# A hybrid convolution and attention block: results stored from ScalarE's queue, loads spread out or issued earlier

## The chip, the cores and the metric

The kernel runs on one core of one Trainium2 chip. The metric is device time of the whole program in microseconds (us), here the median of three runs. Six things work at once: TensorE (PE, with its weight loads PEld), VectorE (DVE), ScalarE (ACT), GpSimd (POOL), the queue of SyncE (SP), which computes nothing and issues DMAs, and the DMA engines that carry the data. Every queue runs in order: an instruction that waits holds up all that stands behind it on the same queue.

## The reference

One block of a diffusion backbone over 2048 tokens of width 1024, with 256 context tokens. In short:

```python
mod = silu(c) @ w_ada + b_ada                    # shifts, scales and gates
h = rms_norm(x) * (1 + sc1) + sh1                # the context likewise
hy, q, k, v, og, gf, gb = split(h @ w_in)
s_f, s_b = final_states(context)                 # start of the recurrences
o = gla(q, k, v, gf, s_f) + reversed gla(..., gb, s_b)     # 4 heads, chunks of 64
y_gla = rms_norm(o) * silu(og)
x0, x1, v = split(short_conv(hy))
y_hy = x0 * (irfft(rfft(x1 * v) * spectrum(filter_mlp)) + bias * (x1 * v))
x = x + g1 * (concat(y_hy, y_gla) @ w_out)
h2 = rms_norm(x) * (1 + sc2) + sh2
x = x + g2 * (square(relu(h2 @ w_mlp1)) @ w_mlp2)
return rms_norm(x) * norm_final
```

The kernel computes all of it in float32 accuracy: matmul operands are split into a high part (`split`: a cast on ACT, line 227) and a low part (a subtraction on DVE, line 228), and three products are summed (lines 222 to 224).

## The kernel before

The work runs in stages, and what one stage hands to the next goes through DRAM tensors: `d_s` (the spectrum of the convolution filter), `d_kt`, `d_v`, `d_og`, `d_q` (per-head operands), `d_u`, `d_x0` (the convolution's inputs), `d_yt` (the mixed output, transposed), `d_h2` (the MLP's input), `d_m` (the MLP's hidden layer). Every DMA in the file, load or store, is issued with `dma = nc.sync.dma_start`, so they all stand on SP's queue in program order.

**Filter and context** (to about 230 us). `mod_dve` (line 425) computes the modulation vectors on DVE: for each of two rows it sums eight terms, and right behind them come the two small matmuls into `pmt` (line 439). `kernel_steps` makes the filter for each of two halves of 256 channels, first generating it (`gen`), then turning it into a spectrum in 16 steps: `fetch` (line 610) loads a table `dff` of the Fourier transform for every second step, `turn` multiplies (`pz`, `pu` line 633), and `second` copies the result to `ks` on ACT (line 636, two buffers) and stores it to `d_s` (lines 640 to 645). `context_steps` is interleaved with it by `run`, which merges streams of work by given costs.

**Projection** (to about 800 us), which fills the DRAM tensors.

**Convolution and attention** (about 800 to 1150 us), two streams merged by `run`: the convolution goes over two halves of the channels, per half a forward part (`uc`, `pa`, `pb`), 16 frequency steps that load `dff`, an inverse table `dfi` and parts of the spectrum `kr`, `ki` (lines 910 to 919), and an inverse part that ends with a product on DVE into `x0` (line 996) and a store of it (line 998). The attention goes over four heads: `load_kv` and `load_q` fetch a head's `kt`, `vv`, `dc`, `qi`, `ki` together after the first quarter of the head before; `outputs` (line 1099) loads the output gate `og` of a quarter and forms `oq` from it; `back` transposes it and stores `yg` (line 1137).

**Output projection**, whose second norm stores `tt` to `d_h2` (line 1309). **MLP, first phase** (1350 to 1950 us): 128 results `c` are formed on ACT and stored to `d_m` (line 1360). **MLP, second phase**: `load_w2` loads and splits a block of weights, `load_u` loads four rows of `d_m`, `split_u` splits them; the phase begins with:

```python
    for kb in range(4):
        load_w2(0, kb)
        if kb == 0:
            load_u(0, 0)
        split_u(0, 0, (kb,))
    load_u(0, 1)
```

Of the kernel before, what the change touches and what calls it, by code (L numbers as in the profile page):

```python
# [10 lines left out]
F32 = mybir.dt.float32  # L11
# [196 lines left out]
def hybrid_block(ctx: ExitStack, tc, a, out, dbg=None):  # L208
    nc = tc.nc
    dma = nc.sync.dma_start  # L210
    mm = nc.tensor.matmul
# [138 lines left out]
    with ExitStack() as ek:  # L350
# [201 lines left out]
        def kernel_steps():  # L552
            for hc in range(2):
# [3 lines left out]

                def gen(t):
                    r = 2 * t
                    pp = pt("pg")  # L560
# [49 lines left out]
                def fetch(t):  # L610
                    kk = 2 * t
                    if t % 2 == 0:
                        st["f", t // 2] = kt_("kd", "dff")
                        dma(st["f", t // 2][:], a["dft_f"][:, kk:kk + 4, :].rearrange("p k n -> p (k n)"))

# [11 lines left out]
                def second(t):  # L627
# [95 lines left out]
    def gates(tbs):  # L723
# [44 lines left out]
        def turn(t):  # L768
# [9 lines left out]
            for h in range(2):  # L778
                dma(d_kt[2 * j + h, :, 4 * tb:4 * tb + 4], kt[h][:])
# [39 lines left out]
    def load_kv(h):  # L819
        kt = pre.tile([P, 16, 2, 64], F32, tag="kt", bufs=1, name="kt")  # L820
        dma(kt[:], d_kt[h])
        vv = gpool(h).tile([P, 16, P], F32, tag="vv", bufs=1, name="vv")
        dma(vv[:], d_v[:, h * P:(h + 1) * P].rearrange("(b p) e -> p b e", p=P))
        heads[h, "kv"] = (kt, vv)
# [50 lines left out]
    def conv_steps():  # L875
        for hc in range(2):
# [29 lines left out]
            def k0(t):  # L906
# [7 lines left out]
                for h in range(2):  # L914
                    hs = slice(h * 64, (h + 1) * 64)
                    dma(kr[hs].rearrange("p (k c) -> p k c", k=2), d_s[kk:kk + 2, 0:64, cs].rearrange("k p c -> p k c"))
# [562 lines left out]
    for kb in range(4):  # L1479
        load_w2(0, kb)  # L1480
        if kb == 0:
            load_u(0, 0)
# [88 lines left out]
```

## Time and profile before

| | |
|---|---|
| time, median of 3 runs | 2693.38 us (2691.67 to 2700.61) |
| profiled execution, its own time | 2698.1 us |
| its span | 2696.3 us |
| mean granted TensorE clock | 0.972 |
| PE busy | 2549.9 us (95%) |
| DVE, ACT, POOL busy | 1384.1, 1045.7, 605.4 us |
| DMA | 353.53 MB, 131 GB/s over the span |

The busy table says which engine is nearest to the span. A row of a stretch has its length, the busy time of each engine with its instructions in brackets, the granted clock (1.00 is 2.4 GHz, 0.50 is 1.2 GHz), the share of the DMA engines and their GB/s; it says where PE isn't busy, and at which clock it ran. The table of waits names for each idle time the work that ended it. The timeline of a queue shows what stood in front of a DMA when it was issued late.

### The profile page before, as it was taken

What the parts mean: (1) busy time and instruction counts of PE and PEld (TensorE: products, weight loads), DVE (VectorE), ACT (ScalarE), POOL (GpSimd) and SP (SyncE); (2) the same over time, 40 slices, a digit from 0 to 9 for tenths busy, and PEclk for the clock granted to TensorE, in tenths of its full rate; (3) what the DMA queues carried; (4) which work ended last, traced back from release to release, by engine and by line L of the source; (5) the groups of instructions that cost most, each with busy time, mean ns of one, the idle gap of its engine ahead of it and who ended that gap; (6) DMA issues with size and microseconds to landing.
All of it is one profiled execution on the core that took longest, in us unless ns stands there. A gap on an engine that the chain in (4) does not pass through costs nothing.

```text
span 2696.3 us, 36126 instructions
## 1 busy us (share of the span) xinstructions
PE 2549.9 (95%) x13704; PEld 2123.2 (79%) x13704; DVE 1384.1 (51%) x2320; ACT 1045.7 (39%) x1863; POOL 605.4 (22%) x568
## 2 busy tenths in 40 slices
PE   9799999999998788899899999999989999999995
PEld 5678978898887677788788887888768888888884
DVE  5755356735567676734543336333344434443654
ACT  6464342225225455334555556555421101111112
POOL 2130231214112213133233233232100000000454
PEclk9899999999999798899999999999999999999998
DMA  5425434432547678656533334333252212221422
GB/s 194 149 78 173 130 129 141 140 113 94 177 149 196 188 214 217 195 171 205 181 108 114 106 114 139 110 114 114 78 183 78 78 48 94 78 79 47 149 98 82
DMA packets 200622, 353.53 MB, mean 131 GB/s; under 512 B 21876, under 2 KB 106744, under 8 KB 192384
## 3 DMA queue, kind: packets, MB, share of 16 engines
q1 hardware_dynamic: 200448, 351.22, 41.0%
q8 instruction: 108, 1.77, 0.3%
q14 instruction: 66, 0.54, 0.1%
HBM read 246.23 MB, written 104.93 MB: 130 GB/s over the span
## 4 chain that ended last, share of the span: by engine, by line
PE 75%; DVE 8%; DMA 7%; issue 4%; POOL 3%; ACT 3%; SPq 0%; POOLq 0%; DVEq 0%; ACTq 0%
PE ps L1340 21%; PE ps L223 7%; PE ps L222 7%; PE ps L224 7%; PE ph L222 3%; PE ph L224 3%; PE ph L223 3%; PE po L223 1%; PE po L224 1%; PE po L222 1%; POOL x L1541 1%; PE pv L222 1%; PE pv L223 1%; PE pv L224 1%; DVE ss L1078 1%
## 5 line engine op out<-in xcount | busy, mean ns | idle before, releaser
L222 PE MATMUL ps<-w2h,uh 128*128 128x512 f32 x1024 | 399.6, 390 | 11.0 <-ACT uh L227 11.0
L223 PE MATMUL ps<-w2l,uh 128*128 128x512 f32 x1024 | 399.2, 390 | 0.2 <-DVE w2l L228 0.2
L224 PE MATMUL ps<-w2h,ul 128*128 128x512 f32 x1024 | 399.1, 390 | 0.0
L1340 PE MATMUL ps<-bh,wh 128*128 128x512 f32 x896 | 352.2, 393 | 9.3 <-ACT wh L227 4.4
L1340 PE MATMUL ps<-bl,wh 128*128 128x512 f32 x896 | 351.6, 393 | 0.3 <-DVE bl L228 0.2
L1340 PE MATMUL ps<-bh,wl 128*128 128x512 f32 x896 | 350.6, 392 | 0.0
L228 DVE TENSOR_TENSOR wl<-raw,wh 128x512 fp32r<-128x512 f32 x217 | 176.7, 820 | 248.9 <-ACT wh L227 248.7
L1538 DVE TENSOR_TENSOR acc<-acc,ps 128x512 f32<-128x512 f32 x192 | 131.8, 686 | 268.2 <-PE ps L224 268.2
L222 PEld LDWEIGHTS ps<-w2h,uh 128*128 128x128 f32 x1024 | 192.8, 188 | 51.3 <-ACT uh L227 11.5
L223 PEld LDWEIGHTS ps<-w2l,uh 128*128 128x128 f32 x1024 | 192.8, 188 | 40.3 <-DVE w2l L228 0.6
L224 PEld LDWEIGHTS ps<-w2h,ul 128*128 128x128 f32 x1024 | 192.6, 188 | 40.4 <-DVE ul L228 0.2
L227 ACT CAST uh<-ur 128x512 fp32r<-128x512 f32 x128 | 70.2, 619 | 367.2 <-PE ps L223 362.4
L1340 PEld LDWEIGHTS ps<-bh,wh 128*128 128x128 f32 x896 | 169.3, 189 | 49.3 <-ACT wh L227 4.8
L227 ACT CAST wh<-raw 128x512 fp32r<-128x512 f32 x217 | 134.2, 623 | 187.3 <-PE ps L1340 152.5
L1340 PEld LDWEIGHTS ps<-bl,wh 128*128 128x128 f32 x896 | 169.7, 189 | 36.7 <-DVE bl L228 1.6
L1340 PEld LDWEIGHTS ps<-bh,wl 128*128 128x128 f32 x896 | 170.0, 190 | 35.5 <-DVE wl L228 0.2
L1547 POOL TENSOR_TENSOR acc<-acc,x 128x1024 f32<-128x1024 f32 x16 | 39.9, 2491 | 632.8 <-PE ps L224 588.4
L222 PE MATMUL ph<-hth,whi 128*128 128x512 f32 x384 | 150.9, 393 | 0.0
L224 PE MATMUL ph<-hth,wlo 128*128 128x512 f32 x384 | 149.6, 390 | 0.4 <-DVE wlo L228 0.4
L222 PE MATMUL pv<-whi,hth 128*128 128x264 f32 x512 | 146.7, 287 | 3.0 <-ACT whi L227 2.9
L223 PE MATMUL ph<-htl,whi 128*128 128x512 f32 x384 | 149.4, 389 | 0.0
L223 PE MATMUL pv<-wlo,hth 128*128 128x264 f32 x512 | 145.0, 284 | 0.3 <-DVE wlo L228 0.3
(282 smaller groups left out, 4980.1 us busy)
## 6 DMA issues: line engine op xcount, KB each, us to landing
d_m<-c SPq DMA_DIRECT2D x128, 256.0 KB, 2.3
ur<-d_m SPq DMA_DIRECT2D x32, 1024.0 KB, 5.3
raw<-in_w_dram SPq DMA_DIRECT2D x31, 1024.0 KB, 5.1
xt<-in_x_dram SPq DMA_DIRECT2D x32, 512.0 KB, 6.9
mwt<-in_wada_dram SPq DMA_DIRECT2D x64, 256.0 KB, 3.0
raw<-in_w_dram SPq DMA_DIRECT2D x32, 512.0 KB, 3.5
raw<-in_wi_vg_dram SPq DMA_DIRECT2D x20, 528.0 KB, 4.9
wada<-in_wada_dram SPq DMA_DIRECT2D x16, 512.0 KB, 7.2
```

Source lines behind the costliest of these rows:

```text
L222: mm(ps, lh, rh, start=first, stop=False)
L223: mm(ps, lh, rl, start=False, stop=False)
L224: mm(ps, ll, rh, start=False, stop=last)
L227: nc.scalar.copy(hi, src)
L228: dve.tensor_sub(lo, src, hi.bitcast(F32))
L1078: dve.scalar_tensor_tensor(ss[64:128, m - 1, :], ss[64:128, m, :], dc[64:128, m:m + 1], ss[64:128, m - 1, :], op0=ALU.mult, op1=ALU.add)
L1340: mm(ps[:], x_[:, sl], y_[:, j, :], start=start and i == 0, stop=stop and i == 2, skip_group_check=True)
L1538: dve.tensor_add(ac, ac, pp[:])
L1541: (dve if at == 31 and p == 3 else gps).tensor_add(x2[:, hs], x2[:, hs], ac)
L1547: gps.tensor_add(acc[:, tile, :], acc[:, tile, :], x2[:])
```

## The change

Five edits, all in the order and the place of DMAs, one also in the order of small matmuls. No arithmetic changes.

1. Stores of results that ACT (or, for `x0`, DVE) has made are issued from ACT's queue: `d_s` (36, four of them small), `d_kt` (16), `d_yt` (16 of `yg`, 4 of `x0`), `d_h2` (32), `d_m` (128), 232 in all. They leave SP's queue.
2. `mod_dve` puts the two matmuls of a row behind the fourth term of the next row. The first two `dff` tables of a half are loaded while its filter is still generated (steps 10 and 12).
3. A head's loads are spread: `kt` after the first quarter of the head before, `vv` behind the `back` that follows, `dc` and `qi` after the second quarter, `ki` behind the `back` that follows. In the convolution the two `kr` loads of a step now stand ahead of its two `ki`.
4. The output gate of a quarter is loaded at the end of the quarter before.
5. The second MLP phase issues its first two blocks of weights and its first `load_u` before the first split.

```diff
+    put_out = nc.scalar.dma_start
...
         def mod_dve(js):
+            ends = []
...
-                    for m in range(2):
-                        o = 4 * j + 2 * m + s
-                        mm(pmt[:, o:o + 1], ac[:, m * P:(m + 1) * P], ones[:, 0:1], start=True, stop=True)
+                        if k == 3 and ends:
+                            ends.pop()()
...
+                    ends.append(end)
+            ends.pop()()
...
                 def gen(t):
                     r = 2 * t
+                    if t in (10, 12):
+                        fetch(t - 10)
...
-                        dma(d_s0[:, cs], k3[127:128, 0, :])
+                        put_out(d_s0[:, cs], k3[127:128, 0, :])
                         dma(d_s[0, 127:128, cs], zrow[0:1, :])
-                        dma(d_s[0, 0:127, cs], k3[0:127, 0, :])
-                        dma(d_s[1, :, cs], k3[:, 1, :])
+                        put_out(d_s[0, 0:127, cs], k3[0:127, 0, :])
+                        put_out(d_s[1, :, cs], k3[:, 1, :])
                     else:
-                        dma(d_s[kk:kk + 2, :, cs].rearrange("k p c -> p k c"), k3)
-
-                yield from staged(16, fetch, turn, second, w=W["k_turn"])
+                        put_out(d_s[kk:kk + 2, :, cs].rearrange("k p c -> p k c"), k3)
+
+                yield from staged(16, lambda t: fetch(t) if t > 3 else None, turn, second, w=W["k_turn"])
...
-                dma(d_kt[2 * j + h, :, 4 * tb:4 * tb + 4], kt[h][:])
+                put_out(d_kt[2 * j + h, :, 4 * tb:4 * tb + 4], kt[h][:])
...
                 if h == 7:
-                    dma(d_yt[ct * P:(ct + 1) * P, :], x0[:])
+                    put_out(d_yt[ct * P:(ct + 1) * P, :], x0[:])
...
     def outputs(h, q):
         vv, qi, ki, ss = heads[h]
         at = heads[h, q // 2]
         b0 = q * 4
-        og = gp.tile([P, 4, P], F32, tag="og", bufs=2, name="og")
-        dma(og[:], d_og[b0 * P:(b0 + 4) * P, h * P:(h + 1) * P].rearrange("(b p) e -> p b e", p=P))
+        if (h, q) == (0, 0):
+            load_og(0, 0)
+        og = heads.pop((h, "og", q))
...
         heads[h, "o", q] = oq
+        if q < 3 or h + 1 < NH:
+            load_og(h + (q + 1) // 4, (q + 1) % 4)
...
-        dma(d_yt[DH + h * P:DH + (h + 1) * P, q * 512:(q + 1) * 512], yg[:])
+        put_out(d_yt[DH + h * P:DH + (h + 1) * P, q * 512:(q + 1) * 512], yg[:])
...
                 outputs(h, q)
+                if q < 2 and h + 1 < NH:
+                    (load_kv, load_q)[q](h + 1, 0)
                 yield W["outs"]
                 if last:
                     back(*last)
                     yield W["back"]
+                if q < 2 and h + 1 < NH:
+                    (load_kv, load_q)[q](h + 1, 1)
                 last = (h, q)
-                if q == 0 and h + 1 < NH:
-                    load_kv(h + 1)
-                    load_q(h + 1)
...
-            dma(d_h2[tb, kp][:, :, p * P:(p + 1) * P], t4)
+            put_out(d_h2[tb, kp][:, :, p * P:(p + 1) * P], t4)
...
-        dma(d_m[2 * n + i, :, tb * 1024 + j * 512:tb * 1024 + (j + 1) * 512], c[:])
+        put_out(d_m[2 * n + i, :, tb * 1024 + j * 512:tb * 1024 + (j + 1) * 512], c[:])
...
+    w2n = [load_w2(0, 0)]
+    load_u(0, 0)
+    w2n.append(load_w2(0, 1))
     for kb in range(4):
-        load_w2(0, kb)
-        if kb == 0:
-            load_u(0, 0)
+        w2n[kb]()
         split_u(0, 0, (kb,))
+        if kb < 2:
+            w2n.append(load_w2(0, kb + 2))
     load_u(0, 1)
```

**Place 1, SP's queue as the spectrum steps of the first half begin.** `xt` are token rows, the number behind a name tells tiles apart. Before:

```order
L325 DMA xt_872<-in_ctx_dram 128x1024
L640 DMA d_s0_58<-ks_855 1x256
L642 DMA d_s_57<-ks_855 127x256
L643 DMA d_s_57<-ks_855 128x256
L325 DMA xt_880<-in_ctx_dram 128x1024
L645 DMA d_s_57<-ks_898 128x2x256
L614 DMA dff_901<-in_dft_f_dram 128x512
L645 DMA d_s_57<-ks_913 128x2x256
L614 DMA dff_929<-in_dft_f_dram 128x512
```

and now:

```order
L326 DMA xt_872<-in_ctx_dram 128x1024
L326 DMA xt_880<-in_ctx_dram 128x1024
L571 DMA dff_901<-in_dft_f_dram 128x512
L326 DMA xt_2022<-in_x_dram 128x1024
L571 DMA dff_929<-in_dft_f_dram 128x512
L326 DMA xt_2030<-in_x_dram 128x1024
L571 DMA dff_957<-in_dft_f_dram 128x512
```

Five stores have left; the second `xt`, the next `dff` and a further `xt` stand directly behind one another.

**Place 2, SP's queue at the change from the first to the second half of the convolution.** From the load of `uc` on. Before:

```order
L828 DMA uc_9010<-d_u_65 128x2048
L1137 DMA d_yt_67<-yg_8697 128x512
L1104 DMA og_8899<-d_og_64 128x4x128
L910 DMA dff_9227<-in_dft_f_dram 128x512
L912 DMA dfi_9229<-in_dft_i_dram 128x512
L916 DMA kr_9231<-d_s_57 64x2x256
L917 DMA ki_9232<-d_s_57 64x2x256
L998 DMA d_yt_67<-x0_8541 128x2048
L823 DMA vv_8969<-d_v_63 128x16x128
```

and now:

```order
L842 DMA uc_9009<-d_u_65 128x2048
L924 DMA dff_9229<-in_dft_f_dram 128x512
L926 DMA dfi_9231<-in_dft_i_dram 128x512
L1120 DMA og_8805<-d_og_64 128x4x128
L930 DMA kr_9233<-d_s_57 64x2x256 x2
L930 DMA ki_9234<-d_s_57 64x2x256 x2
L930 DMA kr_9248<-d_s_57 64x2x256
L837 DMA vv_8971<-d_v_63 128x16x128
```

The store of `yg` and the store of `x0` are gone from between the loads. They stand on ACT's queue, which had here (`zy` are copies for the inverse part, `oq` the attention's):

```order
L980 COPY zy_8743<-py_8738 128x512
L980 COPY zy_8755<-py_8750 128x512
L980 COPY zy_8768<-py_8763 128x512
L1121 ACTIVATE oq_8794<-po_8777 128x512
L980 COPY zy_8810<-py_8805 128x512
```

and has now:

```order
L1163 COPY yg_8699<-pp_8694 128x512
L1164 DMA d_yt_67<-yg_8699 128x512
L994 COPY zy_8745<-py_8740 128x512
L994 COPY zy_8757<-py_8752 128x512
L994 COPY zy_8770<-py_8765 128x512
L1012 DMA d_yt_67<-x0_8543 128x2048
L1146 ACTIVATE oq_8794<-po_8777 128x512
L994 COPY zy_8812<-py_8807 128x512
```

The store of `x0_8543` now stands in front of the `oq` of the next quarter.

**Place 3, SP's queue between the two MLP phases.** Before:

```order
L1360 DMA d_m_70<-c_17015 128x512
L1360 DMA d_m_70<-c_17032 128x512
L1360 DMA d_m_70<-c_17048 128x512
L1459 DMA raw_17063<-in_w2_dram 128x1024
L1467 DMA ur_17069<-d_m_70 128x4x512
L1459 DMA raw_17075<-in_w2_dram 128x1024
L1459 DMA raw_17083<-in_w2_dram 128x1024
L1467 DMA ur_17099<-d_m_70 128x4x512
L1459 DMA raw_17091<-in_w2_dram 128x1024
L1487 DMA nf_17102<-in_norm_final_dram 128x1024
```

and now (`raw_16756` is the last block of first-phase weights):

```order
L1259 DMA raw_16756<-in_w1_dram 128x2048
L1487 DMA raw_17063<-in_w2_dram 128x1024
L1498 DMA ur_17065<-d_m_70 128x4x512
L1487 DMA raw_17067<-in_w2_dram 128x1024
L1487 DMA raw_17077<-in_w2_dram 128x1024
L1498 DMA ur_17099<-d_m_70 128x4x512
L1487 DMA raw_17085<-in_w2_dram 128x1024
L1521 DMA nf_17102<-in_norm_final_dram 128x1024
```

The last stores of the first phase, of which three are shown, no longer stand ahead of the second phase's first loads; `ur` is what `load_u` loads.

## Rows read from the trace of the kernel before

**Rows 1.** The page: busy time of the matrix engine, share of the span, instructions.

```profile
PE 2549.9 (95%) x13704; PEld 2123.2 (79%) x13704; DVE 1384.1 (51%) x2320; ACT 1045.7 (39%) x1863; POOL 605.4 (22%) x568
```

**Rows 2.** Stretches: length, busy time of PE, PEld, DVE, ACT, POOL; granted clock.

```profile
0.00:250.00 250.00, 222.39 (x1435) 172.54 (x1436) 142.48 (x288) 137.14 (x277) 56.25 (x67) 0.95 0.46 147
...
800.00:1150.00 350.00, 292.74 (x2619) 253.21 (x2618) 254.54 (x527) 172.01 (x307) 80.88 (x87) 0.90 0.72 198
...
1350.00:1950.00 600.00, 595.10 (x2586) 488.51 (x2586) 247.90 (x341) 334.18 (x571) 175.61 (x125) 0.99 0.32 110
1950.00:2000.00 50.00, 38.78 (x161) 31.21 (x160) 25.67 (x34) 17.20 (x25) 0.00 (x0) 0.90 0.68 236
```

**Rows 3.** Waits of PE: line, releaser, total us, times, longest us.

```profile
PE pu L938 <- DMA dff<-in_dft_f_dram: 12.7, 2, 8.6
PE ps L222 <- ACT uh L227: 11.0, 1, 11.0
...
PE pu L633 <- DMA dff<-in_dft_f_dram: 9.2, 4, 7.7
PE pd L1063 <- DMA vv<-d_v: 8.2, 1, 8.2
...
PE pc L535 <- DVE ke L527: 6.8, 3, 5.0
...
PE pmt L439 <- DVE ac L435: 4.6, 3, 3.5
...
PE pp L1134 <- DVE oq L1126: 2.4, 1, 2.4
...
PE pa L888 <- DMA uc<-d_u: 1.8, 1, 1.8
```

**Rows 4.** SP's queue in time order: start us, length us, line, DMA.

```profile
94.67 2.28 SPq L643 DMA_DIRECT2D d_s<-ks  x1
...
97.99 0.42 SPq L614 DMA_DIRECT2D dff<-in_dft_f_dram  x1
...
914.93 0.58 SPq L828 DMA_DIRECT2D uc<-d_u  x1
941.78 0.33 SPq L1137 DMA_DIRECT2D d_yt<-yg  x1
...
949.77 0.33 SPq L998 DMA_DIRECT2D d_yt<-x  x1
...
1957.09 0.37 SPq L1467 DMA_DIRECT2D ur<-d_m  x1
```

**Rows 5.** ACT in time order; in brackets its idle time before, and the releaser.

```profile
103.49 0.59 ACT L636 COPY ks<-pu 128x512 f32<-128x512 f32 x1 [4.68 <-DMA d_s<-ks]
...
200.55 0.59 ACT L636 COPY ks<-pu 128x512 f32<-128x512 f32 x1 [3.69 <-DMA d_s<-ks]
...
948.44 0.60 ACT L1121 ACTIVATE oq<-po 128x512 f32<-128x512 f32 x1 [2.25 <-PE po L1118]
...
1955.23 0.63 ACT L1359 ACTIVATE c<-c 128x512 f32<-128x512 f32 x1
1960.59 1.04 ACT L227 CAST w2h<-raw 128x1024 fp32r<-128x1024 f32 x1 [4.73 <-DMA raw<-in_w_dram]
1964.18 2.18 ACT L227 CAST uh<-ur 128x512 fp32r<-128x512 f32 x4 [2.55 <-DMA ur<-d_m]
```

**Rows 6.** The chain of waits: start us, length us, what.

```profile
97.99 7.96 DMA dff<-in_dft_f_dram
...
192.93 7.55 DMA d_s<-ks
...
889.90 8.40 DMA dff<-in_dft_f_dram
```

**Rows 7.** Waits of SP's queue, in the same form as rows 3.

```profile
SPq L998 <- DVE x L996: 21.1, 4, 9.3
```

**Rows 8.** One stretch of the attention stage, columns as in rows 2.

```profile
920.00:930.00 10.00, 9.39 (x44) 8.90 (x44) 7.11 (x18) 2.79 (x6) 0.00 (x0) 0.50 0.23 91
```

More of the change, by code (lines that the diff above doesn't have):

```diff
@@ L436, in mod_dve, with end @@
                         yield 0.33
-                    for m in range(2):
-                        o = 4 * j + 2 * m + s
-                        mm(pmt[:, o:o + 1], ac[:, m * P:(m + 1) * P], ones[:, 0:1], start=True, stop=True)
+                        if k == 3 and ends:
+                            ends.pop()()
+                    def end(ac=ac, o=4 * j + s):
+                        for m in range(2):
+                            mm(pmt[:, o + 2 * m:o + 2 * m + 1], ac[:, m * P:(m + 1) * P], ones[:, 0:1],
+                               start=True, stop=True)
+                    ends.append(end)
+            ends.pop()()
         def mod_end():
@@ L556, in kernel_steps, with fetch @@
                 st = {}
+                def fetch(t):
+                    kk = 2 * t
+                    if t % 2 == 0:
+                        st["f", t // 2] = kt_("kd", "dff")
+                        dma(st["f", t // 2][:], a["dft_f"][:, kk:kk + 4, :].rearrange("p k n -> p (k n)"))
                 def gen(t):
                     r = 2 * t
+                    if t in (10, 12):
+                        fetch(t - 10)
                     pp = pt("pg")
@@ L817, in hybrid_block, with load_kv @@
     gpool = lambda h: gp if h % 2 else pre
[L819 to L824, printed above, removed]
+    def load_kv(h, part=None):
+        if part != 1:
+            kt = pre.tile([P, 16, 2, 64], F32, tag="kt", bufs=1, name="kt")
+            dma(kt[:], d_kt[h])
+            heads[h, "kt"] = kt
+        if part != 0:
+            vv = gpool(h).tile([P, 16, P], F32, tag="vv", bufs=1, name="vv")
+            dma(vv[:], d_v[:, h * P:(h + 1) * P].rearrange("(b p) e -> p b e", p=P))
+            heads[h, "kv"] = (heads[h, "kt"], vv)
     def load_u(ct):
@@ L913, in k0 @@
                 kr, ki = ft("kr", 5, "kr"), ft("ki", 3, "ki")
-                for h in range(2):
-                    hs = slice(h * 64, (h + 1) * 64)
-                    dma(kr[hs].rearrange("p (k c) -> p k c", k=2), d_s[kk:kk + 2, 0:64, cs].rearrange("k p c -> p k c"))
-                    dma(ki[hs].rearrange("p (k c) -> p k c", k=2), d_s[kk:kk + 2, 64:128, cs].rearrange("k p c -> p k c"))
+                for t_, q in ((kr, 0), (ki, 64)):
+                    for h in range(2):
+                        dma(t_[h * 64:(h + 1) * 64].rearrange("p (k c) -> p k c", k=2),
+                            d_s[kk:kk + 2, q:q + 64, cs].rearrange("k p c -> p k c"))
                 if t == 0:
@@ L1035, in hybrid_block, with load_q @@
             gps.memset(az[i][d][:], 0.0)
[L1037 removed]
+    def load_q(h, part=None):
         hr = slice(h * 64, (h + 1) * 64)
[L1039 to L1041 removed]
+        if part != 1:
+            dc = gp.tile([P, 32], F32, tag="dc", bufs=2, name="dc")
+            qi = gp.tile([P, T], F32, tag="qi", bufs=2, name="qi")
+            heads[h, "d"] = (qi, dc)
+        if part != 0:
+            ki = gp.tile([P, T], F32, tag="ki", bufs=1, name="ki")
+            heads[h, "q"] = (heads[h, "d"][0], ki, heads[h, "d"][1])
         for d in range(2):
             ds_ = slice(d * 64, (d + 1) * 64)
[L1044 to L1047 removed]
+            if part != 1:
+                dma(dc[ds_, :], d_dec[d, hr, :])
+                dma(qi[ds_, :], d_q[d, hr, :])
+            if part != 0:
+                dma(ki[ds_, :], d_ki[d, hr, :])
     def states(h):
```

21 lines of the change are left out of this document (7 added, 14 removed).

## The prediction

> **What bounds the kernel now.** The busy table comes first: PE is busy 2549.9 us of a span of 2696.3 [rows 1], so all idle time of PE together is about 146 us, and the change leaves PE's work alone. The stretches come second: they show where those 146 us lie [rows 2]. The first MLP phase (1350 to 1950 us) leaves 4.9 us idle of 600, so a queue that is faster there is worth nothing. The filter stage leaves 27.6 us of 250, the convolution and attention stage 57.3 us of 350 at a granted clock of 0.90, the seam between the MLP phases 11.2 us of 50. Only there can the change pay. The waits of PE come third, since they say what ends each idle time [rows 3]: the tables `dff` (12.7 and 9.2 us), the operands of the second MLP phase (11.0), a head's `vv` (8.2), `ke` (6.8), `pmt` (4.6), `oq` for a transposition (2.4), `uc` (1.8). The timeline of SP's queue and the chain come last: they say whether such a load was late because it was issued late (the change can help) or because its bytes came late (it can't).
>
> **The change part by part.** The sum is made against the profiled execution (2698.1 us, span 2696.3), which lies 4.7 us above the median of 2693.38; I take the saving off the median.
>
> *`mod_dve`.* PE waits 3.5 us at the longest, 4.6 in three waits, for `ac` [rows 3]. The matmuls now come four terms later, so PE's other work can go first. But DVE is the one that is behind, and what needs the sums still waits for them. Between 0 and 3.5 I take 1.5: the wait is moved rather than removed.
>
> *Stores of `d_s`, tables ahead.* Two places. At 94.67 us SP spends 2.28 us to issue a `d_s` store, and the next `dff` is issued at 97.99 [rows 4]; it needs 7.96 us to land [rows 6], and PE waits 7.7 [rows 3]. In the new order the load stands behind two `xt` only (place 1), so it can go some 2.5 us sooner, and no stores are in front of it. Against that, the 2.28 us are now spent by ACT, which has evictions and casts to do there, and `ks` waited 4.68 us for a store's landing, until 103.49 [rows 5]: that is late next, and it bounds the gain at 105.95 (97.99 + 7.96) - 103.49, about 2.5 us, unless the store lands sooner as well. I take 3, with ends -1 and 7.7. At 200.55 ACT has waited 3.69 us for a store to free `ks` [rows 5]; that store was issued at 192.93 and took 7.55 us [rows 6]. `ke` stands behind this eviction on ACT, which gives PE's wait of 5.0 us [rows 3]. The store can start a little sooner, behind its own eviction, and no table is in front of it on its queue. I take 2.5, with ends -1 (ACT's issue time) and 5.0. PE ran at half the clock (0.50) for a while after idle time, as 920 to 930 us shows in the attention stage [rows 8]; each microsecond of it costs PE about half a microsecond. Two microseconds less of it behind these two waits, which is my estimate, are 1 us, with ends 0 and 3.
>
> *Heads' loads, gates and `yg`/`x0` stores.* SP stands still from 915.5 us, when `uc` has been issued, until 941.78, when the `yg` store goes [rows 4]. Behind it stand `og`, `dff`, `dfi`, `kr`, `ki` (place 2). That is 26 us of lead for these loads, but little of it was waited for: the only waits that it explains are `uc` (1.8 us; a head's operands that were held back are loaded beside it) and `oq` (2.4 us, its gate was issued late) [rows 3]. I take 1.8 and 1.5, with lower ends of 0. The great wait, 8.6 us for `dff` [rows 3], is one of bytes: the table was issued at 889.90 and took 8.40 us to land [rows 6], behind a head's `qi` and `ki`. Half of that head's bytes now come later, but they come ahead of the next table, and the number of bytes in this stage, in which the DMA engines are busy 0.72 of the time on average [rows 2], is the same. I take 2, with ends 0 and 8.6. `vv` (8.2) stays where it was, behind the last `ki`; one store less is ahead of it, 0.6 us.
> The price is on ACT. The store of `x0` was issued at 949.77, when DVE had finished; it now stands ahead of an `oq` that ran at 948.44 (place 2) [rows 4, 5]. So that `oq` and the copies behind it start at 949.77 + 0.33, 1.7 us late, and PE's products for the inverse part wait for these copies. The cover is the double buffer of `zy`. I take -1, with ends -2.5 and 0.
>
> *`d_kt`, `d_h2`, `d_m`.* A store of 256 KB costs its queue about 0.33 us [rows 4]. 128 for `d_m` are 42 us on ACT, which is busy 334 of the 600 us there [rows 2] and becomes 376: hidden under PE, 0. SP's long waits for `c` disappear, but no load behind them was late. The output projection has the same trade on a smaller scale: 0, with ends -2 and 0.
>
> *The seam of the MLP.* The last `d_m` stores stood ahead of it on SP, so the first `ur` went out at 1957.09 [rows 4], and PE started 11.0 us late [rows 3]. In place 3 the weights, `ur` and the next weights wait only for buffers that are freed ahead of the first phase's last products, so the data lies there when ACT comes: last square at 1955.23 + 0.63, a store (0.33), the cast of the weights (1.04), the first cast of `ur` (2.18 / 4 = 0.55) [rows 5]: 1955.86 + 0.33 + 1.04 + 0.55 = 1957.8. In the trace the first cast of `ur` started at 1964.18, so it ended at 1964.7: 6.9 us gained. What is late next are the third and fourth weights: they reuse the two buffers, so they can go out only after the first splits, and PE may stand there once more for 1 to 2 us. I take 5, with ends 2 and 7.
>
> Sum: 1.5 + 3 + 2.5 + 1 + 1.8 + 1.5 + 2 + 0.6 - 1 + 0 + 5 = 17.9 us. 2693.4 - 17.9 = 2675.5, rounded to **2675 us**. With the upper ends of all terms (3.5 + 7.7 + 5 + 3 + 1.8 + 2.4 + 8.6 + 0.6 + 0 + 0 + 7 = 39.6) it would be 2654, with the lower ends (0 - 1 - 1 + 0 + 0 + 0 + 0 + 0.6 - 2.5 - 2 + 2 = -3.9) 2697.
>
> The Trainium skill speaks against the stores' new queue: "DMA: Bandwidth & Descriptors", section "Issuing engines are not separate DMA queues", says that DMAs of all issuing engines end on the same 16 DMA engines and interleave, so that issuing on several engines saves only the time to initiate them. By that rule taken literally the stores would be worth 0.33 us each on a queue that PE does not wait for. The trace agrees on the bytes (8.40 us for a table, behind a head's operands) but not on the saving, because 26 us at the `yg` store are a wait for data in front of the issue, and not an initiation.
>
> **The rivals.** *Bytes, not queues.* The loads that PE waits for were limited by what the DMA engines carry and by DVE, and an earlier issue only lets them wait in another place. For it: 8.40 us for a table, `ks` waiting for landings. Against it: the seam, where nothing else was moved by the DMA engines for want of an issue. Then only `mod_dve` at 1.5 and the seam at its lower end of 2 remain: 2693.4 - 3.5 = 2690, within 0.3%. The Trainium skill's rule above would give this outcome.
> *ACT's queue becomes the place where others are held.* ACT is in order; where a store on it waits for DVE or for an earlier DMA that shares its completion counter, the evictions behind it wait too, and PE waits for those. Place: the four `x0` stores and the filter's `d_s` stores. Price: SP waited 21.1 us in four `x0` stores [rows 7], and the slow `d_s` issue of 2.28 us comes once in each half of the filter (4.6), together 25.7 us; the gains of the filter and the attention stage are then gone, and 1.5 and 5 remain. 2693.4 + 25.7 - 6.5 = 2712.6 if all of it reaches PE. It is slower by more than 0.3% (8.1 us) from 14.6 us of held time on. Against it: at the store that I could follow, ACT is held 1.7 us, since it comes late to the store by itself.
> *The clock comes back.* If the 8.6, 7.7 and 5.0 us waits shrink so far that the clock isn't halved after them, the upper ends hold: about 2654, and with the ten microseconds at half speed around 925 us gone (half of it, 5 us) 2649. For it: 0.50 in a stretch in which PE is busy 9.39 of 10 us [rows 8]. Against it: that stretch stands behind a full DMA system.
>
> **How the numbers follow.** The forecast (2660 to 2685) gets 0.60, bytes 0.18, ACT's queue 0.10, the clock 0.12. A measurement of this kernel tells about 0.3% from no change, 8.1 us. Forecast and clock are faster by more than that: 0.72; bytes are the same: 0.18; ACT's queue is slower: 0.10. The range of 2657 to 2692 leaves out most of the clock case and ACT's queue.
>
> **What would show it.** In the changed kernel's trace PE's wait ahead of the second MLP phase should be 4 to 6 us, with ACT in place of the `ur` load as releaser chain; the wait for `dff` near 106 us 3 to 5 us; that for `ke` near 203 us 2 to 3; `uc` and `oq` gone; `vv` still about 8; SP without a wait for `yg`. ACT's longest wait ahead of an eviction should be about 2 us behind the `x0` store. It is wrong if waits of PE for ACT appear that rows 3 doesn't have, or if the `dff` waits keep their size.

## The result, and the profile after

The changed kernel takes 2719.95 us (median of four runs, 2715.25 to 2721.11) against 2693.86 us for the kernel before, measured beside it: ratio 1.0089, 95% interval 1.0068 to 1.0111. It is **slower by 26 us**; the forecast was 2675, with a range of 2657 to 2692. The profiled execution of after (2721.11 us, span 2719.3) can be set against that of before (span 2696.3): 23.0 us.

On the page of after PE is busy 14.0 us longer than before [rows 1] with the same 13704 matmuls, and ACT's DMA ring (q10) carries 62.93 MB that SP's (q1) carried before:

```profile
PE 2563.9 (94%) x13704; PEld 2133.1 (78%) x13704; DVE 1377.3 (51%) x2320; ACT 1047.3 (39%) x1863; POOL 608.5 (22%) x568
...
q1 hardware_dynamic: 151228, 288.29, 33.5%
q10 hardware_dynamic: 49220, 62.93, 6.6%
```

So only 9.0 of the 23.0 us are idle time of PE; the other 14.0 are the same matmuls run more slowly, since the mean granted clock fell from 0.972 to 0.966. Stretches that hold nearly the same matmuls show both in each of the three stages that lose (columns as in rows 2). Filter, attention, output projection before:

```profile
0.00:335.00 335.00, 306.52 (x2093) 252.44 (x2094) 177.62 (x351) 169.19 (x335) 76.63 (x99) 0.96 0.45 144
840.00:1160.00 320.00, 262.96 (x2425) 227.94 (x2424) 232.66 (x466) 155.16 (x278) 80.88 (x82) 0.89 0.73 204
1160.00:1365.00 205.00, 196.26 (x909) 160.68 (x908) 100.04 (x136) 94.13 (x175) 71.91 (x55) 0.98 0.58 184
```

and after:

```profile
0.00:347.00 347.00, 311.95 (x2089) 257.25 (x2090) 176.65 (x350) 168.53 (x333) 79.30 (x98) 0.94 0.43 139
852.00:1179.00 327.00, 269.21 (x2424) 231.28 (x2422) 227.51 (x466) 154.67 (x278) 81.42 (x82) 0.87 0.68 200
1179.00:1394.00 215.00, 199.54 (x910) 163.14 (x909) 98.00 (x136) 94.74 (x176) 70.75 (x57) 0.96 0.54 175
```

PE's idle time (length less busy time) grew by 6.6 us in the filter, 0.8 in the attention stage and 6.7 in the output projection, its busy time by 5.4, 6.3 and 3.3.

To place the whole loss I matched PE's matmuls of the two traces one by one and took how much later each starts than in before; the median of these lags at the end of a stage, less that at the end of the stage before, is what the stage lost, by waits and by the clock together. The same was done for every kernel below:

```
us lost (+) or won (-)   filter   projec-  conv. and  output    1st MLP  seam
against before           to 330   tion     attention  project.  phase
after                     11.8    -0.4       7.3        9.8       1.0    -6.2
ds_on_sp                   0.9    -0.2       1.4       10.0       2.6    -6.0
split127                   3.0    -0.2       4.8        8.9       1.2    -6.1
yt_on_sp                  11.2    -0.8      -6.4        7.6       2.5    -6.3
x0_on_sp                  13.8     0.1       0.8        6.5       2.5    -6.1
yg_on_sp                   8.7    -0.4      -0.2        7.6       2.5    -6.3
h2_on_sp                  12.4     0.2      -1.0        1.3       1.1    -6.2
h2_t7_sp                  11.3     0.1       4.9        4.1       1.1    -6.2
h2_half                   13.4     0.9      -2.8        4.6       2.4    -6.3
combo                     -0.2     0.6      -6.6        1.4       2.3    -6.3
all_sp                     5.4     1.1     -10.1        0.3      -0.1    -0.4
dm_only                    1.9    -1.8     -10.9        0.5       1.4    -6.4
dm_late                    3.4    -3.4      -6.8       -0.8      -1.7    -6.3
b_dm                       1.3     0.5       1.1        0.4       2.3    -6.2
b_w2                       1.6     3.5      -3.2       -0.3      -0.3    -0.9
b_kv                       0.0     0.8      -7.5       -0.6      -0.2    -1.3
kv_late                    5.2    -1.0      -7.3        2.5      -0.1    -6.1
```

Each row is one profiled execution. Kernels whose code is the same in a stage show its scatter: up to 6 us in the filter, 7 in the projection, 10 in the attention stage, 4 or less in the others. A figure is therefore read over all kernels that share the code, and a verdict rests on the timed ratios. The profiled execution of `kv_late` is the longest of its five (2691.50 us at a granted clock of 0.969; the median is 2680.71, and the shortest had 0.977).

PE's waits in after (columns as in rows 3, to be read against them):

```profile
PE pu L952 <- DMA dff<-in_dft_f_dram: 13.8, 4, 7.1
PE ps L1332 <- DVE x L1316: 9.6, 4, 4.7
PE pc L544 <- DVE ke L536: 9.4, 3, 7.4
...
PE pd L1082 <- DMA vv<-d_v: 6.6, 1, 6.6
PE ps L1368 <- ACT wh L228: 5.7, 2, 5.3
PE pp L1161 <- DVE oq L1151: 5.6, 3, 3.2
PE pz L632 <- ACT tt L342: 5.4, 1, 5.4
```

The wait for `dff` in the filter (9.2 us in rows 3) has fallen to 0.3; 5.4 us for ACT's `tt` are new, and `ke` has grown from 6.8 to 9.4. `oq` has grown from 2.4 to 5.6, and the wait at line 1332 (4.1 us at the same place in before) is 9.6.

### The profile page after: what moved, and what is told of

The parts are those of the page before. It is cut to its first block, busy times and chain, and to the rows that moved or that the text cites. A ratio compares the mean times of both kernels' runs of the same rounds, so it can differ in the third digit from the quotient of the medians.

```text
span 2719.3 us, 35891 instructions
## 1 busy us (share of the span) xinstructions
PE 2563.9 (94%) x13704; PEld 2133.1 (78%) x13704; DVE 1377.3 (51%) x2320; ACT 1047.3 (39%) x1863; POOL 608.5 (22%) x568
## 3 DMA queue, kind: packets, MB, share of 16 engines
q10 hardware_dynamic: 49220, 62.93, 6.6%
## 4 chain that ended last, share of the span: by engine, by line
PE 48%; DVE 3%; POOL 3%; DMA 2%; issue 2%; ACT 1%; SPq 0%; POOLq 0%; ACTq 0%; DVEq 0%
PE ps L1368 21%; PE ps L224 8%; PE ps L223 8%; PE ps L225 8%; PE po L224 1%; PE po L225 1%; PE po L223 1%; POOL x L1575 1%; DVE bl L229 1%; DMA raw<-d_h 1%; DMA raw<-in_w_out_dram 0%; DMA d_h<-tt 0%; DVE x L1574 0%; POOL x L1311 0%; POOL mrs L277 0%
## 5 line engine op out<-in xcount | busy, mean ns | idle before, releaser
L225 PE MATMUL pv<-whi,htl 128*128 128x264 f32 x512 | 145.5, 285 | 0.2 <-DVE htl L344 0.2
```

The lines of the kernel that those rows point to most:

```text
L225: mm(ps, ll, rh, start=False, stop=last)
```

## The experiments

### The filter: `d_s` stores

ACT in after, in time order (start us, length us; ACTq rows are DMA issues):

```profile
98.65 0.21 ACTq L653 DMA_DIRECT2D d_s<-ks  x1
98.90 7.47 ACTq L654 DMA_DIRECT2D d_s<-ks  x1
106.42 0.78 ACT L342 ACTIVATE tt<-xp,mod,scl 128x512 f32<-128x512 f32 x1 [7.01 <-issue]
```

The issue behind the store of 127 rows takes 7.47 us, and ACT does nothing else in that time; PE gets its next `pz` operand right after, and then runs at 1.2 GHz (granted 0.51 from 110 to 120 us): four `pu` matmuls take 2.08 us, where they took 1.03 ahead of the wait:

```profile
100.87 1.03 PE L644 MATMUL pu<-zt,dff 128*128 128x256 f32 x4
107.25 1.11 PE L632 MATMUL pz<-prm,zk 128*128 128x128 f32 x4 [5.35 <-ACT tt L342]
108.31 2.08 PE L644 MATMUL pu<-zt,dff 128*128 128x256 f32 x4
```

On SP the same issue had taken 2.28 us [rows 4], and no evictions stood behind it. First run: only the 36 `d_s` stores go back to SP.

```diff
-                        put_out(d_s0[:, cs], k3[127:128, 0, :])
+                        dma(d_s0[:, cs], k3[127:128, 0, :])
...
-                        put_out(d_s[kk:kk + 2, :, cs].rearrange("k p c -> p k c"), k3)
+                        dma(d_s[kk:kk + 2, :, cs].rearrange("k p c -> p k c"), k3)
```

> The changed kernel with the 36 stores of d_s back on SP, all else as changed. Theory A (ACT is held by issuing these stores: one issue took 7.47 us on ACT, and matched matmuls fall behind by 12 us between 85 and 140 us): about 12 us come back, 2720 -> 2708, and the matmuls of the first spectrum steps stand within 2 us of the kernel before. Rival B (the loads brought ahead, xt and dff, take the DMA engines and land late): the 12 us stay, 2718 to 2722.

Measured: 2709.54 us, ratio 1.0052 (1.0032 to 1.0072). The filter loses 0.9 instead of 11.8. The early tables win nothing here: PE's longest wait for `dff` is 7.4 us (7.7 in rows 3), that for `ke` 5.0 as before.

```profile
PE pu L644 <- DMA dff<-in_dft_f_dram: 8.1, 2, 7.4
```

Second run: the stores stay on ACT, and only the one of 127 rows is cut in two.

```diff
-                        put_out(d_s[0, 0:127, cs], k3[0:127, 0, :])
+                        [put_out(d_s[0, r0:r1, cs], k3[r0:r1, 0, :]) for r0, r1 in ((0, 112), (112, 127))]
```

> The changed kernel, but the store of 127 rows of 1 KB, which stands ahead of the slow issue, is cut into 112 and 15 rows, on ACT as changed. Theory A1 (the 127 rows are carried by few of the DMA engines, and the next store's issue on ACT waits for them): the issue behind it falls from 7.47 us to under 1.5, and 6 to 8 us come back, 2712 to 2714. Rival A2 (the issue is slow because the DMA engines are full of loads, whatever the shape): the issue stays over 4 us and the time at 2718 to 2722.

Measured: 2707.42 us, ratio 1.004 (1.0025 to 1.0055), lower than the 2712 to 2714 expected. The issue behind it takes 0.36 us, and the filter loses 3.0:

```profile
97.60 0.81 ACTq L653 DMA_DIRECT2D d_s<-ks  x2
98.75 0.78 ACT L342 ACTIVATE tt<-xp,mod,scl 128x512 f32<-128x512 f32 x1 [0.39 <-DVE htl L344]
98.75 0.36 ACTq L654 DMA_DIRECT2D d_s<-ks  x1
```

So most of the filter's loss is this one shape of store, twice in the program (in the second half the issue takes 1.57 us, and `ke` is 7.45 us late, against 5.0 [rows 3]), and not the number of stores on ACT. With the store cut, the waits for `dff` and `ke` do shrink, to 3.1 and 2.9 us at the longest, but one for `kn` stands beside them (1.0 us in before):

```profile
PE pu L644 <- DMA dff<-in_dft_f_dram: 5.3, 2, 3.1
PE pk L600 <- DVE kn L588: 5.1, 2, 3.3
```

ACT's ring tells why the shape matters. In after, from 102 to 106 us, it moved

```profile
q10 hardware_dynamic: 40, 0.04, 2.9%
```

40 packets of 1 KB in 4 us; with the cut store, from 100 to 102 us,

```profile
q10 hardware_dynamic: 140, 0.12, 17.5%
```

140 in 2 us, seven times the rate. The Trainium skill states the rule behind it, in "DMA: Bandwidth & Descriptors", section "Why a DMA increments its semaphore by 16 and not by 1": a DMA runs on the largest number of DMA engines, at most 16, that divides its outer dimension, and 127 partitions give one. The trace agrees: the 40 packets run one behind the other, while of the 140 up to nine run at a time. The next issue on the queue stands meanwhile, 7.47 us, and 0.36 with the cut. It ended with some 40 of the 127 packets moved, so it did not wait for the whole store; that it waits for room in the ring is my reading. The shape alone doesn't set the price: the same two stores took 1.57 us in the second half.

### The attention stage: `x0` and `yg` stores

Two things are seen in after. First, ACT stands at the `x0` stores until DVE has made `x0`, with work of other streams behind it:

```profile
1115.05 0.33 ACTq L1164 DMA_DIRECT2D d_yt<-yg  x1
1122.87 0.33 ACTq L1012 DMA_DIRECT2D d_yt<-x  x1
1123.24 0.60 ACT L1146 ACTIVATE oq<-po 128x512 f32<-128x512 f32 x1 [8.22 <-DVE x L1010]
```

An `oq` starts 8.22 us late for a product that it doesn't use. Second, SP is not freed by the move: it now stands at the loads of the gates, and loads wait for landings of stores that ACT issued (SP's waits, 840 to 1140 us):

```profile
SPq L1120 <- DVE ss L1097: 54.9, 2, 32.3
...
SPq L930 <- DMA d_yt<-yg: 8.6, 2, 4.9
...
SPq L924 <- DMA d_yt<-yg: 5.7, 1, 5.7
```

In before the largest of these waits was for the results that SP stored itself:

```profile
SPq L1137 <- ACT yg L1136: 48.8, 7, 26.2
```

Its 26.2 us were the lead that the prediction wanted to win; in after SP stands from 932.16 to 954.39 us at the load of a gate, with `kr`, `ki` and `vv` behind it. The profile names DVE as what ended that wait; why the gate's load needed it so late isn't shown. Neither `kr` and `ki` (line 930) nor `dff` (line 924) read or overwrite what a `yg` store touches. In program order `vv` stands behind these `kr`; it is issued at 1069.06, in before at 1049.23:

```profile
1043.46 6.08 SPq L930 DMA_DIRECT2D kr<-d_s  x2
...
1066.47 1.22 SPq L930 DMA_DIRECT2D kr<-d_s  x2
...
1069.06 0.59 SPq L837 DMA_DIRECT2D vv<-d_v  x1
```

Three runs: all 20 `d_yt` stores on SP, the four of `x0` alone, the 16 of `yg` alone.

```diff
-                    put_out(d_yt[ct * P:(ct + 1) * P, :], x0[:])
+                    dma(d_yt[ct * P:(ct + 1) * P, :], x0[:])
...
-        put_out(d_yt[DH + h * P:DH + (h + 1) * P, q * 512:(q + 1) * 512], yg[:])
+        dma(d_yt[DH + h * P:DH + (h + 1) * P, q * 512:(q + 1) * 512], yg[:])
```

> The changed kernel with the 20 stores of d_yt (yg and x0) back on SP. Theory E (stores of x0 ahead of oq hold ACT and cost the attention stage 4 to 8 us): 2712 to 2716. Rival F (the attention stage is bound by bytes and by DVE, the place of these stores is nothing): 2718 to 2722; if they have helped there, 2722 to 2730.

Measured: 2706.65 us, ratio 1.0042 (1.0026 to 1.0057), some 13 us less than after and below the 2712 to 2716 of the theory, which knew the `x0` stores only. PE's wait for `vv` is

```profile
1067.81 1.16 PE L1082 MATMUL pd<-vv,kt 64*128 64x128 f32 x16 [0.95 <-DMA vv<-d_v]
```

> The changed kernel with only the four x0 stores of d_yt on SP, the 16 yg stores on ACT as changed. Theory E1 (ACT is held by the x0 stores, 4.2 and 8.2 us in front of oq): most of what the run with all of d_yt on SP gave back comes back, 2707 to 2711. Theory E2 (the yg stores on ACT's own queue are carried beside the loads that PE waits for, and hold these back): 2715 to 2720, with waits for dff and vv as in the changed kernel.

Measured: 2712.72 us, ratio 1.0057 (1.0044 to 1.007), between the two theories, and `vv` still 6.24 us late.

> The kernel after, with the 16 stores of yg back on SP; the four of x0 and all others stay on ACT. The mirror of the run with the x0 stores on SP. Theory (two costs of their own: x0 holds ScalarE, yg holds the loads on SP until the stores have landed): the attention stage (840 to 1160) falls from +7.3 us to about 0, TensorE's wait for vv from 6.6 to 1 to 2 us, no wait of SP for a yg store over 2 us is left, and ScalarE still stands at the x0 stores for 4 to 8 us each; median near 2712 us. Rival: the waits of SP's loads for yg's landings come of the bytes in flight and not of the queue that issues the stores; then vv stays near 6.6 us and the time within 2 us of after.

Measured: 2713.8 us, ratio 1.0073 (1.005 to 1.0096), an interval that overlaps that of after. No load of SP waits for a `yg` store (with all 20 on SP it was 0 to 0.6 us in five kernels), so the wait goes with the queue that issues the store and not with its bytes; an `oq` still stands 7.2 us behind an `x0` store; `vv` is at 4.8 us, not the 1 to 2 expected:

```profile
1067.45 2.08 PE L1082 MATMUL pd<-vv,kt 64*128 64x128 f32 x16 [4.80 <-DMA vv<-d_v]
```

Over the table: six kernels with all `d_yt` stores on ACT lie at -2.8 to 7.3 (mean 2.4), five with all on SP at -6.4 to -10.9 (mean -8.2), so the 20 stores cost about 11 us. With either half alone on ACT it is 0.8 and -0.2, as if one half were enough to lose most of it; but these are single executions of a stage with 10 us of scatter, and by the timed ratios the `x0` stores give back 0.0032 and the `yg` stores 0.0016 of the 0.0047 that both give back. How the 11 us divide is not settled. That SP's waits come of a completion counter that DMAs of both queues use is my reading; the trace shows the wait and its releaser only.

### The output projection: `d_h2` stores

On GpSimd in after, the sum into `x` (line 1311) stands behind additions on raw weights (lines 1260 to 1262) that had to wait:

```profile
1283.09 1.29 POOL L1260 TENSOR_TENSOR raw<-raw 128x512 f32<-128x512 f32 x1 [7.70 <-issue]
1284.45 1.63 POOL L1261 TENSOR_TENSOR raw<-raw 128x512 f32<-128x512 f32 x1
1286.05 1.73 POOL L1262 TENSOR_TENSOR raw<-raw 128x512 f32<-128x512 f32 x1
1287.74 2.83 POOL L1311 TENSOR_TENSOR x<-x,xt 128x1024 f32<-128x1024 f32 x1
```

In before the sum came first:

```profile
1261.27 2.78 POOL L1283 TENSOR_TENSOR x<-x,xt 128x1024 f32<-128x1024 f32 x1 [5.14 <-DVE x L1282]
1264.83 1.30 POOL L1232 TENSOR_TENSOR raw<-raw 128x512 f32<-128x512 f32 x1 [0.79 <-DMA raw<-in_w_dram]
```

and PE waits 4.72 us for what follows from the sum:

```profile
1306.72 0.69 PE L1332 MATMUL ps<-prm,x 128*128 128x128 f32 x2 [4.72 <-DVE x L1316]
```

No line of the diff touches GpSimd; its order differs all the same, and the runs below show that it follows the queue of four `d_h2` stores. Three runs part this from the issue of the stores, 0.52 us each on ACT: all 32 on SP (GpSimd in the order of before), only the four of `t == 7` on SP (GpSimd in the order of before), and the 16 of `t >= 8` on SP (GpSimd in the order of after).

```diff
-            put_out(d_h2[tb, kp][:, :, p * P:(p + 1) * P], t4)
+            dma(d_h2[tb, kp][:, :, p * P:(p + 1) * P], t4)
```

> The changed kernel with the 32 stores of d_h2 back on SP; with that the order of GpSimd at the first w1 block is that of the kernel before again (the residual sum ahead of the weight sums). Theory C (the output projection loses 9 to 10 us through these stores, by the order they bring on GpSimd or by their 0.52 us of issue on ACT): 2720 -> 2710 to 2712, and matched matmuls lose under 2 us between 1250 and 1370. Rival D (it is the late start of that stage and other loads): 2718 to 2722.

Measured: 2706.23 us, ratio 1.0032 (1.0021 to 1.0043), lower than expected; the stage loses 1.3 instead of 9.8.

> The changed kernel with 4 of the 32 stores of d_h2 (those of the eighth token block) on SP, 28 on ACT as changed. GpSimd's order at the first w1 block is then that of the kernel before. Theory C1 (the output projection lost 8 to 9 us because a residual sum on GpSimd stood behind weight sums that waited for their load): time as with all of d_h2 on SP, 2705 to 2710. Theory C2 (ACT's issue of these stores, 0.52 us each and in order, is the loss): 28 of 32 remain, 2716 to 2720.

Measured: 2710.19 us, ratio 1.0044 (1.0029 to 1.0058); 4.1 us, and PE's longest wait at line 1332 is 2.0.

> The kernel after, with the 16 stores of d_h2 of t >= 8 on SP and the 16 of t < 8 on ACT; GpSimd's instructions stand in the order of after. Theory: the loss of the output projection (9.8 us from 1160 to 1320) is mostly the order on GpSimd, 5 to 6 us, and 4 us the issue of 32 stores on ACT: it falls to 7 to 8 us, and TensorE still waits at line 1332 behind GpSimd's residual sum. Rival: it goes with the number of stores on ACT: it falls to 4 to 5 us.

Measured: 2712.52 us, ratio 1.0065 (1.0046 to 1.0084); 4.6 us, outside the 7 to 8 expected and where the rival had it. But line 1332 still waits, which the rival doesn't explain:

```profile
PE ps L1332 <- DVE x L1316: 7.3, 4, 4.3
```

The lags inside the stage settle it. With GpSimd's order of after, 4.2 to 6.2 us are lost between about 1262 and 1300 us (after 5.4, `h2_half` 4.6), without it 0.8 and 1.0. With the stores of `t >= 8` on ACT, another 3.1 to 4.7 are lost from there to the end of the stage (after 3.7, `h2_t7_sp` 3.5), without them 0.1 and 0.8. So there are two causes, and they add up; the second lies wholly in the later half, which my expectation had spread evenly. That it is the 0.52 us of each issue is not shown by itself.

### The MLP's seam: `d_m` stores, and all stores together

With every other store of the loss back on SP (`d_s`, `d_yt`, `d_h2`), and with all 232 there:

> The changed kernel with d_s, d_yt and d_h2 stored from SP again (d_kt and d_m from ACT, all edits of the loads kept). Sum of what the single runs gave back by matched matmuls: filter +1 against the kernel before, attention -6 (from the run with d_yt on SP), output projection +1 (from the run with d_h2 on SP), first MLP phase +1 to +2, seam between the MLP phases -6: about -9, 2684 to 2688 and faster than both. Rival (the gifts overlap: without the stores' new place the loads' edits are worth nothing): 2692 to 2698.

Measured: 2689.29 us, ratio 0.9973 (0.996 to 0.9986), just above the 2684 to 2688 expected.

> The changed kernel with all 232 stores on SP: only the loads' edits and the later pmt matmuls are left. Theory (the seam's gain of 6 us needs the d_m stores away from SP, since the second phase's loads stand behind the last of them there): 5 to 6 us slower than the run with d_s, d_yt and d_h2 alone on SP, with PE's wait at the second phase's start near 10 us again. Rival (the seam's gain comes from the new order of its loads): the same time as that run, and that wait near 4 us.

Measured: 2689.86 us, ratio 0.9975 (0.9965 to 0.9986). Both beat the kernel before. The time is not 5 to 6 us above `combo`, as expected, but the same, as the rival had it; in the table `all_sp` wins back in the attention stage and the first phase what it lacks at the seam. The wait sides with the theory. PE's wait ahead of the second phase is in `combo`

```profile
PE ps L223 <- ACT uh L228: 4.1, 1, 4.1
```

and in `all_sp`, where the loads of the second phase have their new order,

```profile
PE ps L223 <- ACT uh L228: 11.1, 1, 11.1
```

So the gain at the seam needs `d_m` off SP. Four runs ask which part of it: `d_m` alone on ACT, the last eight `d_m` stores alone on ACT (the edit below, against `all_sp`), and in the kernel before only the `d_m` stores or only the new order of loads.

```diff
-        dma(d_m[2 * n + i, :, tb * 1024 + j * 512:tb * 1024 + (j + 1) * 512], c[:])
+        (put_out if tb and n < 2 else dma)(d_m[2 * n + i, :, tb * 1024 + j * 512:tb * 1024 + (j + 1) * 512], c[:])
```

> The kernel after, with all stores back on SP but those of d_m; the edits of the loads are kept. Theory: what the loads' edits and the seam bring add up, since they lie in different stages: about -5 to -10 us by the end of the attention stage as in the kernel with all stores on SP, then +2 us in the first MLP phase (1645 to 1680, as in the kernel with d_m and d_kt on ACT), and -6 us at the seam with a wait of TensorE ahead of the second phase near 4 us. Sum -9 to -13 us against before, about 2682 to 2688 us. Rival: the seam's gain is eaten by the loss in the first MLP phase and by the filter stage; then it lies with the kernel with all stores on SP, at 2690 us.

Measured: 2686.47 us, ratio 0.9969 (0.9954 to 0.9984); the seam's -6.4 and 1.4 us lost in the first phase, as expected.

> As the kernel with only d_m on ACT, but of the 128 stores of d_m just the last eight (units n = 1 and 0 of the second half of the columns) on ACT. Theory: the seam is decided by the stores that are last in SP's queue, so TensorE's wait ahead of the second phase falls to about 4 us as with all 128, and the 1 to 2 us lost at 1645 to 1680 stay away, unless those come of another cause: about 2680 to 2687 us. Rival: the loads of the second phase are held by stores farther back in SP's queue; then the wait stays near 11 us and the time near 2690 us.

Measured: 2684.18 us, ratio 0.9962 (0.9947 to 0.9976). By the matched matmuls eight stores win the whole 6.3 us, and the first phase loses nothing; the timed interval still overlaps that of `all_sp`.

> The kernel before, with the 128 d_m stores on ACT and nothing else. Theory: the seam's gain comes of the store's queue alone: TensorE's wait ahead of the second phase falls from 11.0 to 4 to 6 us, the first MLP phase loses 1 to 2 us, total -3 to -6 us (about 2689 us). Rival: the new order of the second phase's loads is what shortens the wait, or both are needed; then the wait stays at 9 to 11 us and the time is 0 to +2 us against before.

Measured: 2694.95 us, ratio 0.9995 (0.9982 to 1.0007): the wait falls to 4.1 us, the seam wins 6.2, the first phase loses 2.3, and in the timed runs no gain can be told (3 to 6 us were expected).

> The kernel before, with the new order of the second phase's first loads (two tiles of w2 and u's first operand ahead of the splits) and nothing else. Theory: the loads stand behind the d_m stores in SP's queue whatever their order, so TensorE's wait ahead of the second phase stays near 11 us and the time within 1.5 us of before. Rival: the order alone brings the wait to 4 to 6 us and the time to about 2688 us.

Measured: 2697.92 us, ratio 1.0004 (0.9989 to 1.0019), the wait still

```profile
PE ps L222 <- ACT uh L227: 11.1, 1, 11.1
```

The order of the loads is worth nothing that this run can tell; what stands ahead of them on SP is.

### Which edits of the loads pay

`all_sp` and its relatives win 6 to 11 us in the attention stage. Only the spread of a head's loads, put into the kernel before:

```diff
+                if q < 2 and h + 1 < NH:
+                    (load_kv, load_q)[q](h + 1, 0)
                 yield W["outs"]
...
+                if q < 2 and h + 1 < NH:
+                    (load_kv, load_q)[q](h + 1, 1)
                 last = (h, q)
-                if q == 0 and h + 1 < NH:
-                    load_kv(h + 1)
-                    load_q(h + 1)
```

> The kernel before, with a head's loads (kt, vv, qi, ki) spread over steps and nothing else. Theory: in the kernels with the stores on SP 5 to 8 us are won between 1020 and 1110, where the 8.2 us wait for vv stood; the spread loads bring them: the wait for vv falls to 1 to 3 us and the time by 4 to 7 us, to about 2690 us. Rival (as the prediction had it): vv lands when SP's earlier loads let it, and the wait only goes to the next load; then vv stays near 8 us, or dff's wait grows by what vv loses, and the time is within 2 us of before.

Measured: 2685.67 us, ratio 0.9971 (0.996 to 0.9982), a little more than the 4 to 7 us expected, though `vv`'s wait stays above the expected 1 to 3 us. `vv` is issued at 1045.50 instead of 1049.23, a gate and `dc` stand behind it where four large `qi` and `ki` loads stood, the first of which now follows 5.8 us later instead of 0.5, and PE has `vv` 7.6 us earlier (before, then `b_kv`):

```profile
1061.56 2.08 PE L1063 MATMUL pd<-vv,kt 64*128 64x128 f32 x16 [8.23 <-DMA vv<-d_v]
```

```profile
1053.96 2.08 PE L1071 MATMUL pd<-vv,kt 64*128 64x128 f32 x16 [4.03 <-DMA vv<-d_v]
```

The states `ss` are formed from `vv`, and PE's wait for them falls with it:

```profile
PE po L1118 <- DVE ss L1078: 6.2, 1, 6.2
```

```profile
PE po L1126 <- DVE ss L1086: 1.8, 1, 1.8
```

4.2 and 4.4 us, of which the wait for `dff` takes back 1.9 (12.7 before, 14.6 now), make up most of the 7.5 that the stage wins. Of the 7.6 us 3.7 are the earlier issue; that the other 3.9 come of the bytes which no longer follow at once is argued and not shown. Last, this edit with the last eight `d_m` stores on ACT, and nothing else of the change (the edit is against `b_kv`):

```diff
+    put_out = nc.scalar.dma_start
...
-        dma(d_m[2 * n + i, :, tb * 1024 + j * 512:tb * 1024 + (j + 1) * 512], c[:])
+        (put_out if tb and n < 2 else dma)(d_m[2 * n + i, :, tb * 1024 + j * 512:tb * 1024 + (j + 1) * 512], c[:])
```

> The kernel before, with a head's loads spread over steps and the last eight d_m stores (units n = 1 and 0 of the second half of the columns) on ACT; no other edit. Theory: the two gains lie in different stages and add up, about -6.5 us by 1160 and -6.5 us at the seam, -13 us in all, about 2682 us, and the other five edits of the change (gates of the output, d_s stores, tables, the tables' products, the order of w2's loads) bring nothing by themselves. Rival: the edits of the other loads bring 3 us or more; then the time stays 3 us or more above that of the kernel with all edits of the loads and the last eight d_m stores on ACT (2684 us, ratio 0.9962).

Measured: **2680.71 us, ratio 0.9944 (0.993 to 0.9958)**, 14.5 us faster than before and the lowest of all. The two gains add up, and the edits of the change that it leaves out bring nothing that these runs can tell (`dm_late`, with all edits of the loads: 0.9962, intervals overlap).

## Why the prediction was wrong

The rival "ACT's queue becomes the place where others are held" came true (it had a chance of 0.10 and 2712.6 us), with its places, but that its total came so near is partly luck: it priced the `x0` stores at 21.1 us, where all 20 `d_yt` stores cost about 11, and the `d_s` stores at 4.6 (the second issue took 1.72 us, so 4.0), where 11.8 were lost, and it had nothing for `d_h2` and for the waits on SP. Step by step, predicted gain against the table:

- **`d_s` stores, tables, `mod_dve`, clock: 8.0 predicted (1.5 + 3 + 2.5 + 1), 11.8 lost.** The step that failed is the price of the issue on ACT: I set the lower end at -1 and took 2.28 us from SP's row [rows 4]. On ACT it was 7.47 us, under which evictions for PE waited. The clock's term had the wrong sign: 1 us was to be won, and PE, granted 0.94 instead of 0.96, was busy 5.4 us longer with the filter's matmuls. Nor was there the tables' gain: with `d_s` on SP the filter wins nothing (-0.2 to 5.4 lost in five kernels), since the longest wait for `dff` is still 7.3 to 7.7 us there; with the 127 rows cut on ACT that wait and the one for `ke` shrink as forecast, and the one for `kn` takes their place, as the first rival had it.
- **`uc`, `oq`, `dff` and the `x0` price: 1.8 + 1.5 + 2 - 1 = 4.3 predicted, with `vv` 4.9; 7.3 lost (mean of six kernels 2.4).** The `x0` stores were judged by the one that I could follow (1.7 us); in after two of them hold ACT by 4.17 and 8.22 us. SP's wait for `yg`, said to go, came back at the loads of the gates (54.9 us, against 48.8) and as the wait of loads for landings of `yg` (8.6 and 5.7 us), so the lead for `dff`, `kr` and `ki` was not won. In the two profiled executions nearly all that this stage lost is the clock: PE is idle 0.8 us longer and busy 6.3 us longer. The rows for `uc` (2.8) and `dff` (13.8) did not shrink.
- **`vv`: 0.6 predicted, 7.5 measured** where the stores don't hide it (`b_kv`). I looked at what stands ahead of `vv` on SP, and neither at its own earlier place nor at the 2 MB of `qi` and `ki` behind it; and the 6.2 us for `ss`, which hang on `vv`, I had not counted.
- **`d_h2`: 0 predicted (-2 to 0), 9.8 lost.** I priced the issue and missed that the store's queue changes the order of work on GpSimd.
- **`d_m`: 0 predicted, 1.0 to 2.6 lost** where all 128 stand on ACT: in `b_dm` PE waits 4.1 us once for a weight's low part near 1675 us.
- **The seam: 5 predicted (2 to 7), 6.2 won**, the wait 4.1 us (4 to 6 predicted). The mechanism was right, though the credit belongs to eight stores and none to the order of the loads.

The Trainium skill's rule that I weighed ("DMA: Bandwidth & Descriptors", section "Issuing engines are not separate DMA queues") came nearer than my sum for 224 of the 232 stores: moving them won nothing. At the seam the trace differs: eight stores at 0.33 us to issue are 2.6 us, and 6.3 were won, because what they saved was a place in an in-order queue. The price on the engine that issues, here 7.47 and 8.22 us, is not in that rule.

What would have told it: place 2 shows a DMA on ACT's queue ahead of evictions, and such a place should have been priced by the longest wait that SP has in that line (9.3 us for `x0`, [rows 7]; 8.22 came), not by the one that is easiest to follow.

## What to carry to other kernels

A store on a compute engine's queue costs that engine the wait for its data and the wait behind a slow store, and all its work behind them; moved away from SP, it may free SP less than it seems, because the next load in line can wait as long. Leave stores on SP unless a load that is waited for stands right behind them, and then move those few alone. Before moving any, look for stores whose number of rows divides badly, as 127 does, and look at the order on the engines that the diff doesn't touch. When a load comes late, look at what shares the DMA engines behind it as well as at what is issued ahead of it. Price a wait of PE with the slower matmuls that follow it: here they were more than half of the loss.

## What the runs showed of the hardware

- A store of 127 rows of 1 KB moved 40 packets in 4 us; cut into 112 and 15 rows, ACT's ring moved 140 in 2 us. The 40 ran one behind the other. Behind the first, the next issue on the same queue took 7.47 us, behind the second 0.36.
- Loads on SP waited 14.3 us in all (8.6 and 5.7) for landings of `yg` stores issued on ACT, with which they share no data; with these stores on SP it was 0 to 0.6 us in six kernels (`yg_on_sp`, `yt_on_sp`, `combo`, `all_sp`, `dm_only`, `dm_late`).
- The same matmuls of the attention stage kept PE busy 262.96 us at a mean granted clock of 0.89 and 269.21 us at 0.87; behind an idle time of 5.35 us four `pu` matmuls took 2.08 us, ahead of it 1.03.
